# Seven products for a part of z, behind the first feed-forward, and new stage offsets

## The chip, the cores and the metric

The kernel runs on one NeuronCore of a Trainium2 chip. A core has TensorE (PE, matmuls), VectorE (DVE), ScalarE (ACT), GpSimd (POOL) and SyncE (SP, which issues nearly all transfers here), each with its own instruction stream, kept in step by semaphores. The metric is the time of one execution on the device in microseconds, the median of several.

## The reference

One layer of a decoder trunk over 2048 tokens of width 1024, in fp32: a gated DeltaNet mixer of 8 heads beside a memory cross-attention of 4 heads, then a squared-ReLU feed-forward, with a layer norm behind each. What matters for the change is the projection z, the gate of the mixer:

```python
def gdn_mixer(x, mem_k, mem_v, w_in, conv_w, a_log, dt_bias, gate_norm_w, w_out):
    proj = x @ w_in                                  # x: 2048 x 1024
    qkv = proj[..., :3 * GDN_WIDTH]
    z = proj[..., 3 * GDN_WIDTH:4 * GDN_WIDTH]       # 1024 columns, 128 to a head
    ...
    qkv = jax.nn.silu(causal_depthwise_conv(qkv, conv_w))
    ...
    o = chunk_gated_delta_rule(q, k, v, g, beta)     # state carried from chunk to chunk
    o = (rms_norm(o, gate_norm_w) * jax.nn.silu(heads(z))).reshape(B, T, GDN_WIDTH)
    m = memory_attention(mq, mem_k, mem_v)
    return jnp.concatenate([o, m], axis=-1) @ w_out

x = layer_norm(ALPHA * x + mix, ln1_g, ln1_b)
x = layer_norm(ALPHA * x + sqrelu_mlp(x, w_ff1, w_ff2), ln2_g, ln2_b)
```

z doesn't depend on the recurrence, so it can be computed at any time before the gate is applied.

## The kernel before

**Precision.** Every large product is made of three matmuls in fp32r: each operand is split into a high and a low part (ACT casts the high part, DVE subtracts it for the low one), and `mm3` adds high x high, high x low and low x high in PSUM. A wide matmul is 128 x 128 weights times 512 columns.

**Stages.** The 2048 tokens are four blocks of 512 (b = 0 to 3), and two blocks are a superblock (s = 0, 1). For each superblock the program runs the mixer of its two blocks, then the output projection (`out_seven`), the feed-forward's first half (`ff1`) and its second half (`ff2`). In the trace the first superblock takes from 0 to 1367 us, and its `ff2` from 1057 to 1367; the mixers of blocks 2 and 3 run from 1367 to 1942.

**Seven products.** `out_seven`, `ff1` and `ff2` multiply 2 x 2 blocks of matrices by seven products in place of eight (table `SEVEN`, L1190): sums and differences of the operands' quadrants (A11 to A22 and S1 to S4 of the tokens, B11 to B22 and T1 to T4 of the weights) are made by DVE beforehand, kept in DRAM, and loaded and split when their product comes. `quad_sums` (L1202) makes those of weights. In `ff2` each of the seven takes 192 wide matmuls (PSUM tiles f2A, f2B, f2C), in eight steps of 24; step u loads tokens (X, or xh and xl in the seventh product) and weights (whl).

**The mixer.** `mixer` (L1677) goes through ten steps t. Step t makes q, k and v of head t (`dense`: three projections of 24 wide matmuls, PSUM tiles aq, ak, av), the chunk-local part of head t-1 (`gdn_a`, `invert`: transposes ptk, ptq, ptv, products pkq, and the small products pq, pp in fp32), the recurrence of head t-2 (`gdn_b`: pc, po, pto), z of head t-1 (`gate`, L843: 24 wide matmuls into az, then tanh on ACT and one DVE instruction into cz), and in four steps a memory head (amq, sps, pmT, pmo). In blocks 1 to 3 the split weights are loaded from wsc in DRAM, where block 0 has put them. Between these, ACT, DVE and POOL do the convolution, the norms and the inverse.

**What sets the order.** The program is recorded, not issued, as it is written; `Recorder.issue` (L336) then lays all instructions out engine by engine. It gives each a cost and a time at which its operands would be ready, and at each point takes, of the instructions that could start, the one of the lowest priority number. That number is the place in the written order plus a stage offset from the table `PLACE` (`spot`, L552; `o.prio`, L245): (2, 4, 'Z') is z in step 4 of block 2. The chip then runs each engine's stream strictly in that order. SP is such a stream too: a transfer that waits for a free buffer holds up those behind it.

**Buffers that matter here.** Tag "d" has 11 tiles of 128 x 512, tag "s0" 14, whl 4 (each the high and low part of 128 x 1024), the token tiles "tt" 8; PSUM has 8 banks (acc 3, ga0, ga1, pb 2, m).

All instructions of the recorder have one line in the profile, L447, so rows are told apart by their tiles.

Of the kernel before, what the change touches and what calls it, by code (L numbers as in the profile page):

```python
# [14 lines left out]
P = 128  # L15
# [169 lines left out]
class Op:  # L185
# [278 lines left out]
def hybrid_layer(  # L464
# [378 lines left out]
    def gate(b, h, T):  # L843
        a = bank("az", "acc")
        project(a, load_in(b, ZO // P + h), T)
        c = slot("cz", "d")
        th = slot("th", "th")
        nc.scalar.activation(th, a, AF.Tanh, scale=0.5)
        nc.vector.scalar_tensor_tensor(out=c, in0=th, scalar=1.0, in1=a, op0=ALU.add, op1=ALU.mult)
        return c  # L850
# [327 lines left out]
    MEM_AT = {5: 0, 6: 1, 7: 2, 8: 3}  # L1178
# [320 lines left out]
    def ff2(s, x1d):  # L1499
# [58 lines left out]
        for n, (xn, wn, bn, on, (th, nh)) in enumerate(SEVEN):  # L1558
# [18 lines left out]
            for u in range(HU - LT):  # L1577
# [5 lines left out]
                if n == 3 and u in (2, 3):  # L1583
                    affine(*((ln2_g, "kq0"), (ln2_b, "kq1"))[u - 2])
                rec.gate = None
# [19 lines left out]
            if xn == "S1":  # L1605
                for t in range(NC):
                    norm2(NC + t)
# [331 lines left out]
```

## Time and profile before

| | us |
|---|---|
| Median of 3 runs | 2705.01 (2702.50 to 2705.70) |
| The profiled execution | 2702.34 |
| Its span, first to last instruction | 2700.6 |
| PE busy | 2685.2 (99%) |
| DVE busy | 2087.0 (77%) |
| ACT busy | 1624.8 (60%) |
| POOL busy | 423.3 (16%) |
| Bytes moved | 613.79 MB, mean 227 GB/s |
| Granted TensorE clock | 0.999 (2.4 GHz) |

The profile's busy share is a union of spans: two instructions that overlap in an engine's pipeline count once. A row of the timeline joins equal instructions that follow each other; its start, and the start of the next row, tell how long the run held the engine. A wait is listed with the engine that stood still, and with what ended it.

### The profile page before, as it was taken

The page shows a single profiled execution, that of the slowest core. Times are in us where ns is not written, and L with a number is a line of the kernel's source. Part 1 is how long each engine was busy: PE and PEld are TensorE (multiplying, and loading weights), DVE is VectorE, ACT ScalarE, POOL GpSimd, SP SyncE. Part 2 cuts the span into 40 slices and gives each one's busy share as a digit, 9 for nine tenths or more (in the row PEclk, how much of TensorE's full clock was granted, in tenths as well). Part 3 has the DMA queues.
Part 4 walks back from the last instruction along what each step waited for, and adds up shares of the span by engine and source line. Part 5 has one row for each costly group of instructions (what it writes and reads, how often), then busy time and mean ns, then how long its engine had stood idle before and what let it go on. Part 6 is the DMA issues. An engine that isn't in the chain of part 4 may idle for free.

```text
span 2700.6 us, 42393 instructions
## 1 busy us (share of the span) xinstructions
PE 2685.2 (99%) x13577; PEld 2248.5 (83%) x13577; DVE 2087.0 (77%) x5604; ACT 1624.8 (60%) x4098; POOL 423.3 (16%) x1023
## 2 busy tenths in 40 slices
PE   9999999999999999999999999999999999999998
PEld 7888888888888888888888888888887888888887
DVE  7998889998867776756778888789977656667575
ACT  7778777776575555334446776578756655544341
POOL 3333133331000000000032221233201000000001
PEclk9999999999999999999999999999999999999999
DMA  8676659868788888765664444444678644586673
GB/s 317 235 258 207 234 178 311 300 233 285 276 307 289 293 302 287 270 215 189 234 222 157 151 150 175 175 162 138 238 271 290 206 138 153 171 293 216 215 237 114
DMA packets 209070, 613.79 MB, mean 227 GB/s; under 512 B 24112, under 2 KB 32720, under 8 KB 188880
## 3 DMA queue, kind: packets, MB, share of 16 engines
q1 hardware_dynamic: 208416, 611.04, 65.0%
q8 instruction: 107, 1.75, 0.3%
q14 instruction: 115, 0.94, 0.1%
q10 hardware_dynamic: 432, 0.05, 0.0%
HBM read 436.35 MB, written 174.65 MB: 226 GB/s over the span
## 4 chain that ended last, share of the span: by engine, by line
PE 96%; DVE 2%; ACT 1%; DMA 0%; issue 0%; POOL 0%; POOLq 0%; ACTq 0%; DVEq 0%
PE f2A L447 13%; PE fA L447 13%; PE ao L447 8%; PE az L447 7%; PE fC L447 6%; PE f2C L447 6%; PE av L447 6%; PE ak L447 6%; PE aq L447 6%; PE fB L447 3%; PE f2B L447 3%; PE amq L447 3%; PE pc L447 3%; PE po L447 2%; PE pkq L447 2%; PE pq L447 1%
## 5 line engine op out<-in xcount | busy, mean ns | idle before, releaser
L447 DVE TENSOR_TENSOR whl<-wraw,whl 128x512 fp32r<-128x512 f32 (+2 forms) x294 | 256.9, 884 | 102.6 <-ACT whl L447 99.9
L447 ACT CAST whl<-wraw 128x512 fp32r<-128x512 f32 (+2 forms) x294 | 226.2, 780 | 182.6 <-PE fC L447 73.5
L447 PE MATMUL fA<-B,whl 128*128 128x512 f32 x1152 | 286.4, 389 | 0.0
L447 PE MATMUL f2A<-whl,X 128*128 128x512 f32 x1152 | 263.1, 389 | 0.0
L447 ACT CAST X<-X 128x1024 fp32r<-128x1024 f32 x118 | 124.1, 1052 | 228.1 <-DMA X<-xsc 174.6
L447 PEld LDWEIGHTS fA<-B,whl 128*128 128x128 f32 x1152 | 216.2, 188 | 45.0
L447 PEld LDWEIGHTS f2A<-whl,X 128*128 128x128 f32 x1152 | 216.3, 188 | 44.9
L447 DVE TENSOR_TENSOR X<-X,X 128x1024 fp32r<-128x1024 f32 x118 | 143.8, 1221 | 130.2 <-ACT X L447 130.0
L447 PE MATMUL az<-T,whl 128*128 128x512 f32 x768 | 215.9, 406 | 0.0
L447 PE MATMUL ak<-T,whl 128*128 128x512 f32 x768 | 213.4, 405 | 0.6 <-ACT cq L447 0.5
L447 PE MATMUL aq<-T,whl 128*128 128x512 f32 x768 | 210.6, 404 | 0.5 <-DVE T L447 0.4
L447 PE MATMUL av<-T,whl 128*128 128x512 f32 x768 | 209.3, 403 | 0.0
L447 PE MATMUL fC<-B,whl 128*128 128x512 f32 x768 | 196.9, 389 | 0.0
L447 PE MATMUL f2C<-whl,X 128*128 128x512 f32 x768 | 174.7, 389 | 0.0
L447 PEld LDWEIGHTS fC<-B,whl 128*128 128x128 f32 x768 | 144.1, 188 | 30.1 <-DVE B L447 0.2
L447 PEld LDWEIGHTS f2C<-whl,X 128*128 128x128 f32 x768 | 144.2, 188 | 29.9
L447 POOL TENSOR_SCALAR ve<-mv 128x1 f32<-128x1 f32 x34 | 15.6, 460 | 915.0 <-DVE mv L447 915.0
L447 PEld LDWEIGHTS aq<-T,whl 128*128 128x128 f32 x768 | 136.7, 189 | 25.3 <-DVE T L447 2.3
L447 PEld LDWEIGHTS ak<-T,whl 128*128 128x128 f32 x768 | 137.1, 189 | 24.3 <-ACT cq L447 0.6
L447 PEld LDWEIGHTS av<-T,whl 128*128 128x128 f32 x768 | 137.4, 189 | 23.2
L447 PEld LDWEIGHTS az<-T,whl 128*128 128x128 f32 x768 | 136.5, 189 | 22.4
L447 PE MATMUL ao<-whl,X 128*128 128x512 f32 x528 | 139.7, 403 | 0.0
(296 smaller groups left out, 6260.8 us busy)
## 6 DMA issues: line engine op xcount, KB each, us to landing
whl<-wsc SPq DMA_DIRECT2D x108, 1024.0 KB, 4.9
wraw<-in_w_ff_dram SPq DMA_DIRECT2D x106, 512.0 KB, 4.3
X<-xsc SPq DMA_DIRECT2D x96, 512.0 KB, 3.9
wsc<-whl SPq DMA_DIRECT2D x36, 1024.0 KB, 6.0
whl<-tsc SPq DMA_DIRECT2D x64, 512.0 KB, 4.8
xsc<-hB SPq DMA_DIRECT2D x96, 256.0 KB, 3.1
xo<-cat SPq DMA_DIRECT2D x80, 256.0 KB, 3.3
wraw<-in_w_in_dram SPq DMA_DIRECT2D x35, 512.0 KB, 5.9
```

What stands on the lines that cost most here:

```text
L447: o.fn(*[res(a) for a in o.args], **{k: res(v) for k, v in o.kw.items()})
```

## The change

Three things change.

1. z of heads 0 to 3 in blocks 2 and 3 is no longer made in the mixers. The tokens of blocks 2 and 3 (th = 0, 1) are the rows, and heads 0, 1 and 2, 3 (nh = 0, 1) the columns of a 2 x 2 problem, with the 1024 inputs halved; seven products of 24 wide matmuls make it, in a new function `gate_seven` that stands behind the first superblock's `ff2`. Its gated result goes to DRAM (zsc), and `gate` in the mixers loads it from there.
2. The sums that it needs are made in `ff2` of the first superblock, at six places (`SUMS_AT`) in its third, fourth and fifth product: of weights into zws, of tokens into zxs.
3. The table of stage offsets is another one throughout. The memory heads of block 3 stand one step later (`MEM_AT`), the first weights of block 2 are loaded behind `gate_seven`, and the last norms of `ff2`'s second half have small offsets.

```diff
@@ PLACE: 176 offsets before, 215 now, nearly all with other values
-    ('w',): 140, (0, 0, 'D'): 5, (0, 0, 'F'): -5, (0, 0, 'H'): -585, (0, 1, 'D'): -70, (0, 1, 'F'): 75,
+    (None,): 190, ('w',): 70, (0, 0, 'D'): 50, (0, 0, 'H'): -210, (0, 1, 'D'): -225, (0, 1, 'H'): 145,
...
     def gate(b, h, T):
+        if b in Z_BLOCKS and h < 2 * ZH:
+            c = slot("cz", "d")
+            nc.sync.dma_start(out=c, in_=zsc[b, h])
+            return c
         a = bank("az", "acc")
...
-    MEM_AT = {5: 0, 6: 1, 7: 2, 8: 3}
+    MEM_AT = {b: {5 + (b == 3) + h: h for h in range(MH)} for b in range(NB)}
...
@@ in ff2, before step u of product n
+                if s == 0 and (n, u) in SUMS_AT:
+                    spot(n, u, "zS")
+                    i = SUMS_AT.index((n, u))
+                    (gate_weight_sums if i < ZH else gate_token_sums)(i if i < ZH else i - ZH)
+                    spot(None)
...
             if xn == "S1":
                 for t in range(NC):
+                    rec.shift = 30 + 45 * t
                     norm2(NC + t)
+                rec.shift = 0
...
+    Z_BLOCKS = (2, 3)
+    ZH = 2
+    SUMS_AT = ((2, 0), (2, 4), (3, 0), (3, 3), (3, 6), (4, 1))
...
+    def gate_token_sums(k):
+        a11, a12, a21, a22 = (slot("xq", "d") for _ in range(4))
+        for b, lo, hi in zip(Z_BLOCKS, (a11, a21), (a12, a22)):
+            for x, kk in ((lo, k), (hi, k + KT // 2)):
+                nc.sync.dma_start(out=x, in_=xtd[:, kk, b * TB:(b + 1) * TB])
+        nc.sync.dma_start(out=zxs["A22"][:, k].part(k), in_=a22)
+        sub(a22, a21, a22, ALU.add)
+        sub(a21, a11, a21)
+        sub(a11, a22, a11)
+        sub(a12, a12, a11)
+        for n, x in (("S1", a22), ("S3", a21), ("S2", a11), ("S4", a12)):
+            nc.sync.dma_start(out=zxs[n][:, k].part(k), in_=x)
...
+    def gate_seven(T):
+        K2 = KT // 2
+        def tokens(n):
+            if n in ("A11", "A12"):
+                ks = range(K2 * (n == "A12"), K2 * (n == "A12") + K2)
+                return [(T_of(T, 0, k), T_of(T, 1, k)) for k in ks]
+            x = []
+            for k in range(K2):
+                hi, lo = slot("xh", "d", F32R), slot("xl", "s0", F32R)
+                split_in_place(hi, lo, zxs[n][:, k].part(k))
+                x.append((hi, lo))
+            return x
...
+        def finish(th, nh, j, a, c):
+            g = slot("th", "th")
+            nc.scalar.activation(g, a, AF.Tanh, scale=0.5)
+            nc.vector.scalar_tensor_tensor(out=c, in0=g, scalar=1.0, in1=a, op0=ALU.add, op1=ALU.mult)
+            nc.sync.dma_start(out=zsc[Z_BLOCKS[th], nh * ZH + j], in_=c)
...
+        for n, (xn, wn, bn, on, q) in enumerate(SEVEN):
+            spot(n, 0, "zX")
+            x = tokens(xn)
+            spot(n, 0, "zW")
+            w = weights(wn)
+            spot(None)
...
+            for j in range(ZH):
+                a = banks[bn][j]
+                for k in range(K2):
+                    c = slice(k * P, (k + 1) * P)
+                    mm3(a, w[j][0][:, c], w[j][1][:, c], *x[k], k == 0 and not on, k == K2 - 1, skip_group_check=on)
+                if q == (0, 1):
+                    finish(*q, j, a, slot("cz", "d"))
+                elif (q, j) not in met:
...
+                    nc.scalar.copy(out=held[q, j], in_=a)
+                else:
+                    sub(held[q, j], a, held[q, j], ALU.add)
+                    finish(*q, j, held[q, j], held[q, j])
...
         ff2(s, x1d)
+        if s == 0:
+            gate_seven(ahead["T"])
+            ahead["w0"] = load_in(Z_BLOCKS[0], 0)
```

What this does to the order is seen at three places. The first is PE at the end of the first superblock's `ff2`: f2A is its last product, T the split tokens of block 2 (two numbers, high and low), aq the first projection of block 2's mixer, az a product of z. Before:

```order
L447 MATMUL f2A<-whl,xh 128x512 x2
L447 MATMUL f2A<-whl,xl 128x512
L447 MATMUL aq<-T_14640,whl 128x512
L447 MATMUL aq<-T_14652,whl 128x512
L447 MATMUL aq<-T_14640,whl 128x512 x2
```

And now, with a piece left out in which the first product goes on:

```order
L454 MATMUL f2A<-whl,xh 128x512 x2
L454 MATMUL f2A<-whl,xl 128x512
L454 MATMUL az<-T_14761,whl 128x512
L454 MATMUL az<-T_14771,whl 128x512
L454 MATMUL az<-T_14761,whl 128x512 x2
...
L454 MATMUL az<-xh,whl 128x512
L454 MATMUL az<-xl,whl 128x512
```

Where the mixer began, z begins: first on the tokens T, then on the loaded sums xh and xl. 147 of its 168 matmuls stand in one run; the other 21, of the seventh product, stand between the first two heads' projections.

The second place is SP at the same stage: xl is a token tile as it lands, whl weights, xj and wraw are what the next block's tokens and the feed-forward's weights land in. Before:

```order
L447 DMA xj<-in_xt_dram 128x512 x2
L447 DMA whl<-wsc 128x2048
L447 DMA xl<-xsc 128x512 x8
L447 DMA wraw<-in_w_ff_dram 128x1024
L447 DMA xj<-in_xt_dram 128x2x512 x3
L447 DMA scr<-gct 32x128
```

And now:

```order
L454 DMA xl<-xsc 128x512 x8
L454 DMA xl<-zxs 128x512 x2
L454 DMA xj<-in_xt_dram 128x2x512
...
L454 DMA whl<-wsc 128x512 x4
L454 DMA xl<-zxs 128x512
L454 DMA scr<-gct 32x128
L454 DMA out_dram<-y 128x512 x2
L454 DMA xl<-zxs 128x512
L454 DMA whl<-zws 128x1024
```

Seven token loads for the seven products stand between the feed-forward's last token loads and the weights of the first product; the others follow, among writes of the output.

The third is PE in block 2's mixer, where head 0's z stood: ptk and ptq are transposes of a head's k and q. Before:

```order
L447 MATMUL az<-T_14694,whl 128x512
L447 MATMUL ptk<-ident,ck 128x128 x4
L447 MATMUL az<-T_14683,whl 128x512 x2
...
L447 MATMUL az<-T_14823,whl 128x512
L447 MATMUL ptq<-ident,cq 128x128 x4
L447 MATMUL az<-T_14817,whl 128x512 x2
```

And now:

```order
L454 MATMUL aq<-T_14793,whl 128x512
L454 MATMUL ptk<-ident,ck 128x128 x4
L454 MATMUL aq<-T_14802,whl 128x512
...
L454 MATMUL aq<-T_14929,whl 128x512
L454 MATMUL ptq<-ident,cq 128x128 x4
L454 MATMUL aq<-T_14935,whl 128x512
```

The transposes that stood among z's matmuls stand among the next head's first projection. In numbers of instructions over the whole program: PE 12495 before and 12471 now; DVE's TENSOR_TENSOR 2499 and 2553; ACT's casts and copies 1735 and 1765; SP's DMAs 1410 and 1506.

## Rows read from the trace of the kernel before

**Rows 1.** The page, busy us (share of the span) and instructions.

```profile
PE 2685.2 (99%) x13577; PEld 2248.5 (83%) x13577; DVE 2087.0 (77%) x5604; ACT 1624.8 (60%) x4098; POOL 423.3 (16%) x1023
```

**Rows 2.** The page, the chain that ended last, by engine.

```profile
PE 96%; DVE 2%; ACT 1%; DMA 0%; issue 0%; POOL 0%; POOLq 0%; ACTq 0%; DVEq 0%
```

**Rows 3.** Waits of PE: us in total, times, longest us.

```profile
PE ao L447 <- ACT whl L447: 1.4, 4, 0.6
PE warm L447 <- POOL mhalf L534: 1.2, 1, 1.2
...
PE pp L447 <- POOL at L447: 0.2, 1, 0.2
```

**Rows 4.** Windows: us, PE, PEld, DVE, ACT, POOL busy, clock, DMA share, GB/s.

```profile
0.00:310.00 310.00, 306.69 (x1710) 256.42 (x1710) 273.77 (x954) 240.58 (x709) 102.51 (x234) 1.00 0.72 254
310.00:610.00 300.00, 299.13 (x1740) 255.92 (x1739) 275.42 (x1083) 223.88 (x777) 99.31 (x244) 1.00 0.72 251
...
1057.00:1276.00 219.00, 219.00 (x968) 181.41 (x967) 132.49 (x141) 86.81 (x86) 2.85 (x6) 1.00 0.69 235
...
1367.00:1650.00 283.00, 283.00 (x1612) 241.46 (x1610) 231.85 (x923) 193.24 (x667) 81.85 (x232) 1.00 0.48 171
1650.00:1942.00 292.00, 291.71 (x1673) 249.32 (x1674) 248.00 (x982) 207.66 (x726) 85.30 (x213) 1.00 0.49 172
```

**Rows 5.** Timeline of PE in ff2: start us, us, instructions joined.

```profile
1189.52 43.68 PE L447 MATMUL f2C<-whl,X 128*128 128x512 f32 x192
1233.04 43.68 PE L447 MATMUL f2A<-whl,X 128*128 128x512 f32 x192
```

**Rows 6.** Timeline of PE in the mixer of block 2.

```profile
1377.65 5.60 PE L447 MATMUL av<-T,whl 128*128 128x512 f32 x24
1383.10 1.30 PE L447 MATMUL aq<-T,whl 128*128 128x512 f32 x5
...
1402.28 1.98 PE L447 MATMUL az<-T,whl 128*128 128x512 f32 x8
1404.10 0.60 PE L447 MATMUL ptk<-ident,ck 128*128 128x128 f32 x4
1404.46 3.03 PE L447 MATMUL az<-T,whl 128*128 128x512 f32 x12
1407.33 0.60 PE L447 MATMUL ptq<-ident,cq 128*128 128x128 f32 x4
1407.68 1.17 PE L447 MATMUL az<-T,whl 128*128 128x512 f32 x4
1408.69 1.98 PE L447 MATMUL aq<-T,whl 128*128 128x512 f32 x8
```

**Rows 7.** Windows of three other stretches, columns as in rows 4.

```profile
490.00:520.00 30.00, 29.40 (x168) 24.93 (x166) 28.95 (x106) 21.62 (x70) 12.00 (x29) 1.00 0.95 351
1189.00:1232.00 43.00, 43.00 (x192) 35.60 (x191) 21.42 (x21) 16.54 (x16) 0.00 (x0) 1.00 0.67 220
...
1367.00:1400.00 33.00, 33.00 (x158) 27.64 (x157) 25.24 (x43) 19.91 (x60) 13.78 (x31) 1.00 0.78 304
```

**Rows 8.** Timeline of PE in out_seven of superblock 1, transposes.

```profile
2059.78 0.27 PE L447 MATMUL pt<-ident,y 128*128 128x128 f32 x1
...
2060.58 0.71 PE L447 MATMUL pt<-ident,y 128*128 128x128 f32 x5
```

**Rows 9.** DVE: z's gate from 1367 to 1942; the sums, ns min/median/max.

```profile
L447 DVE SCALAR_TENSOR_TENSOR cz<-th,az 128x512 f32<-128x512 f32 x16 | 10.9, 682 | 2.8 <-ACT th L447 2.7
L447 DVE TENSOR_TENSOR wq<-wq x88: 637/685/748, 308.3 to 1030.5; 128x512 f32<-128x512 f32 x88
```

**Rows 10.** Tile xl: cast, subtraction (ns min/median/max), landing.

```profile
L447 ACT CAST xh<-xl x68: 603/620/644, 644.3 to 2664.1; 128x512 fp32r<-128x512 f32 x68
L447 DVE TENSOR_TENSOR xl<-xl,xh x68: 642/686/694, 645.6 to 2664.8; 128x512 fp32r<-128x512 f32 x68
...
DMA to landing us min/median/max: 3.0/6.2/8.1
```

More of the change, by code (lines that the diff above doesn't have):

```diff
@@ L1606, in ff2 @@
                 for t in range(NC):
+                    rec.shift = 30 + 45 * t
                     norm2(NC + t)
+                rec.shift = 0
+    Z_BLOCKS = (2, 3)
+    ZH = 2
+    SUMS_AT = ((2, 0), (2, 4), (3, 0), (3, 3), (3, 6), (4, 1))
+    zsc = {(b, h): rec.buf(dr, (P, TB), F32, "zsc%d%d" % (b, h), 1, "zsc") for b in Z_BLOCKS for h in range(2 * ZH)}
+    zws = {n: rec.buf(dr, (P, ZH * TB), F32, "zws" + n, 1, "zws") for n in ("T1", "T2", "T3", "T4")}
+    zxs = {n: rec.buf(dr, (P, KT // 2, TB), F32, "zxs" + n, 1, "zxs") for n in ("S1", "S2", "S3", "S4", "A22")}
@@ new lines, in gate_weight_sums @@
+    def gate_weight_sums(j):
+        w = [w_in[ZO // P + j + ZH * nh] for nh in range(2)]
+        quad_sums([slot("wq", "d") for _ in range(4)],
+                  {(h, nh): w[nh][:, h * TB:(h + 1) * TB] for h in range(2) for nh in range(2)},
+                  {n: zws[n][:, j * TB:(j + 1) * TB] for n in zws}, 0)
+    def gate_token_sums(k):
[10 more added lines that the diff above has]
+            nc.sync.dma_start(out=zxs[n][:, k].part(k), in_=x)
@@ new lines, in gate_seven, with weights @@
+    def gate_seven(T):
[10 more added lines that the diff above has]
+            return x
+        def weights(n):
+            w = []
+            for jp in range(ZH // 2):
+                t, hi, lo = pair()
+                if n[0] == "T":
+                    split_in_place(hi, lo, zws[n][:, jp * 2 * TB:(jp + 1) * 2 * TB].part(2 * jp, 2 * jp + 1))
+                else:
+                    h, nh = int(n[1]) - 1, int(n[2]) - 1
+                    for i in range(2):
+                        for u, v in enumerate((hi, lo)):
+                            c = slice(u * 1024 + h * TB, u * 1024 + (h + 1) * TB)
+                            nc.sync.dma_start(out=v[:, i * TB:(i + 1) * TB].bitcast(F32),
+                                              in_=wsc[ZO // P + 2 * jp + i + ZH * nh][:, c])
+                w += [(hi[:, i * TB:(i + 1) * TB], lo[:, i * TB:(i + 1) * TB]) for i in range(2)]
+            return w
+        def finish(th, nh, j, a, c):
[3 more added lines that the diff above has]
+            nc.sync.dma_start(out=zsc[Z_BLOCKS[th], nh * ZH + j], in_=c)
+        tags = {"A": ("ga0", "ga1", "pb", "pb"), "B": ("acc", "acc", "acc", "m")}
+        tags["C"] = tags["B"]
+        banks, held, met = {}, {}, set()
+        for n, (xn, wn, bn, on, q) in enumerate(SEVEN):
[4 more added lines that the diff above has]
+            spot(None)
+            if not on:
+                banks[bn] = [bank("az", g) for g in tags[bn]]
+            for j in range(ZH):
[6 more added lines that the diff above has]
+                elif (q, j) not in met:
+                    met.add((q, j))
+                    if j % 2 == 0:
+                        t = tok_tile("z")
+                        for i in range(2):
+                            held[q, j + i] = t[:, i * TB:(i + 1) * TB].part(i)
+                    nc.scalar.copy(out=held[q, j], in_=a)
+                else:
+                    sub(held[q, j], a, held[q, j], ALU.add)
+                    finish(*q, j, held[q, j], held[q, j])
@@ L1672, in next_block @@
         else:
-            ahead["w0"] = load_in(b, 0)
+            if b != Z_BLOCKS[0]:
+                ahead["w0"] = load_in(b, 0)
             ahead["G"] = gates(b, ahead["ab"])
@@ L1695, in mixer @@
             spot(b, t, "M")
-            if t in MEM_AT:
-                h = MEM_AT[t]
+            if t in MEM_AT[b]:
+                h = MEM_AT[b][t]
                 c = cat_tile()
```

67 rows, old and new, of the table PLACE are left out of this document.

## The prediction

> **What bounds the kernel now.** I read the page's busy times first [rows 1]: PE is busy 2685.2 us of 2700.6, DVE comes next with 77%. The chain of waits says the same in another way [rows 2]: 96% of what ended last is PE. The waits of PE alone [rows 3] are ten entries that add up to 6.6 us; the remaining idle time, 15.4 - 6.6 = 8.8 us, is the last normalisation after the last product. So PE hardly ever stands still, and what shortens the kernel is fewer or cheaper PE instructions, or up to 6.6 us of waits.
>
> The windows by stage [rows 4] show who is second where. In the mixers of blocks 2 and 3 (1367 to 1942) PE idles 0.29 us of 575 and DVE is busy 231.85 + 248.00 = 479.85 us, 83%. In the mixers of blocks 0 and 1, DVE is at 88% and 92%, and PE idles 3.31 and 0.87 us. So a mixer can run with 92% of DVE and still cost PE only 0.3% of its time. In the feed-forward's second half DVE is at 60%.
>
> A busy PE need not be PE at its peak, so the price of a matmul is read from starts. An unbroken run of 192 products starts at 1189.52 and the next group at 1233.04 [rows 5]: 43.52 / 192 = 0.2267 us for one matmul of 512 columns. In a mixer a run of 24 goes from 1377.65 to 1383.10 [rows 6], 0.227 again. PE is at its own rate in both places; the 83% of PEld [rows 1] is what such a run shows as well (35.60 of 43.00 us, [rows 7]).
> The Trainium skill (Trace Analysis, section Identifying the Most-Contended Engine) says that matmul occupancy is a bad measure of headroom and that the busy share of weight loads should be used; by that 17% of PE would be free, the removed matmuls would sit on spare time, and the result would be 2702.3 us, no gain. The unbroken run with 83% of weight loads disagrees: there is no hole in it to take up, so I go by the rows and keep the rule as a small rival.
>
> **The change, part by part.**
> 1. Removed on PE: z of heads 0 to 3 in blocks 2 and 3 is 2 x 4 x 8 x 3 = 192 matmuls; the seven products are 7 x 2 heads x 4 x 3 = 168. That is 24 x 0.2267 = -5.44 us. They all are on the path, since PE is.
> 2. New order on PE. I counted in the two orders how often PE goes back from small fp32 products to the wide ones: 709 times before, 736 now. Price of one: head 0's z in block 2 starts at 1402.28 and the next projection at 1408.69 [rows 6]; within these 6.41 us stand 24 wide matmuls (5.45) and two groups of four transposes, so a group costs 0.48. Five transposes in a row take 0.71 and one 0.27 [rows 8], so one more costs 0.11 and four cost 0.44. An interruption itself is 0.04 us; 27 x 0.04 = +1.1 us. Bounds: 0, and 27 x 0.48 = 13 if the whole group were extra work, which it isn't, because the number of transposes is the same.
> 3. Added to DVE and ACT, behind the first superblock's feed-forward. DVE gets 54 more subtractions: 24 for the sums of weights and tokens (0.685 each as the wq rows, [rows 9]), 20 splits of tokens (0.69, [rows 10]), 4 splits of weights at twice that width, and 6 joins; about 40 us in all. ACT gets 30 casts and copies, about 20 us. The 24 sums (16 us) fall in the second half of the feed-forward, where DVE has 86 us free [rows 4]. The rest, 24 us, and the 8 gates of z that come here from the mixers (8 x 0.682, [rows 9]) fall beside 38.1 us of seven products (168 x 0.2267). In the 33 us that follow the feed-forward now, DVE was busy 25.24 [rows 7]; together 55 of 71 us. Hidden. Were it not hidden, the whole 29 us could show.
> 4. The mixers of blocks 2 and 3 lose 192 x 0.2267 = 43.5 us of PE work as cover and only 8 x 0.682 of DVE's [rows 9]. DVE then is busy 474.4 of 531.5 us, 89%. Between the two mixers that show 88% and 92% [rows 4]: block 1's idle share, 0.29%, gives 1.5 us of idle, block 0's (with the program's start in it) 5.7. I take 1.5, which is +1.2 on the 0.29 us there now. The order supports it: the transposes of k and q that stood among z's matmuls stand among the next head's aq now, with 12 wide matmuls between them, as before.
> 5. Added DMAs: 96 on SP. Of these, 52 are the sums, 13.6 MB within about 100 us from the third of the seven feed-forward products on. The stretch moves 220 GB/s now [rows 7], so it will ask for about 350. The seven products load 5.2 MB of tokens, 5.2 MB of weights and store 2.1 MB, 12.5 MB; with the 10 MB of the 33 us that follow now (304 GB/s, [rows 7]) that is 22.5 MB in 71 us, 317 GB/s. The mixer stretch at 490 us moves 351 GB/s with PE idle 0.60 of 30 us [rows 7]: 2% of idle is the nearest row, 2 us over the first stretch if its look-ahead weren't there. The token loads of the feed-forward run four steps ahead of PE (tag "tt", eight buffers, two a step), so I take 0, and keep the 2 us as an end.
> The Trainium skill (DMA: Bandwidth & Descriptors, section Specifications) puts HBM's limit at about 358 GB/s for a core; by it the first stretch would just fit, which changes no term. The trace's 351 GB/s over 30 us is in accord.
> 6. SP's queue. Between the last feed-forward loads and the first mixer weights now stand 20 token loads, each of which waits for a free slot. Tag "d" has 11 slots, 2.75 products of four. A load that is issued when a product ends has 1.75 x 5.44 = 9.5 us until its use. It needs 6.2 us to land (median; the longest 8.1), 0.62 on ACT and 0.69 on DVE [rows 10]: 7.5 us, 9.4 at worst. It fits by 2 us. Behind a late one wait the weights of the next product and, after them, of the first mixer.
> 7. The offsets elsewhere: the number of PE instructions in each other stage is the same, and only 6.6 us of PE waits are there to win or to double. I take 0, with -5 and +5 as ends.
>
> Sum: -5.4 + 1.1 + 1.2 = -3.1 us. The profiled execution took 2702.34 us (its span is 2700.6), so the sum gives 2699.2 on it. It lies below all three timed runs (2702.50 to 2705.70, median 2705.01); on their median the sum gives 2701.9. I forecast a median between these, nearer to the latter: 2701.4 us.
>
> **The rivals.**
> (a) The new offsets also recover waits. For it: 6.6 us of waits are listed, and no reason protects them. Against it: they are ten small entries, the longest 1.2 us, and at the program's start the order barely changes. With all of them halved, another -3.3 us: 2698; with all of them gone, 2695.
> (b) The cover is gone: with 43.5 us less PE work in the mixers, DVE sets their pace here and there. At block 0's idle share, 5.7 us come in place of 1.5, and the sum is +1.1: about 2706 on the median, no change. DVE at 100% isn't reached (474 of 531), so it can't be more by this way alone.
> (c) The seven products starve; this ends on the slower side. PE takes them in their written order, 147 z matmuls in one run, so a token tile that comes late stops PE with nothing to fill in. The place is the 38 us behind the feed-forward; the point from which it decides is a load-to-use time over 9.5 us. If the look-ahead shrinks to one product, each of the five products with token sums waits 7.5 - 5.4 = 2.1 us: +10.5. Then 2705.0 - 3.1 + 10.5 = 2712. For it: SP's queue is in order, and writes of the output that wait for the normalisation stand among these loads. Against it: the first product needs no loaded tokens, and seven of the token loads stand ahead of its weights.
> (d) The change doesn't do what it says: the wide matmuls sit on spare PE time, and nothing is gained. 2705. Only the weight-load share speaks for it.
>
> **How the numbers follow.** A measurement of this kernel can tell about 0.2% (5.4 us) from no change, so faster means under 2699.6 us and slower over 2710.4. The forecast (a gain of 1 to 6 us) has 0.55, of which 0.10 lie under 2699.6. Rival (a) has 0.22, nearly all faster. Rival (b) has 0.09, all within. Rival (c) has 0.11, nearly all slower. Rival (d) has 0.03. So faster 0.32, within 0.57, slower 0.11. Eight times in 10 the time should lie between 2694 (rival (a) with all the waits gone) and 2712 (rival (c)); the forecast's own range is 2698 to 2705.
>
> **What would show it.** Wide matmuls: 9960 in place of 9984, with the unbroken runs still at 0.2267. The stage behind the feed-forward: seven products in about 38 us with no PE wait on xl, xh or whl; waits of 2 us there, about five, would be rival (c). Mixers 2 and 3 together, without the seven products: about 533 us, with DVE near 89% and PE idle under 2 us; 4 us or more would be rival (b). The ten PE waits: a total of 3 us or less would be rival (a). The prediction is wrong if the seven products end but the mixers don't get shorter by some 43 us, or if another stage, above all the first two mixers, moves by more than 3 us.

## The result, and the profile after

The changed kernel takes 2709.82 us, the kernel before 2703.55 us in the same session (medians of 12 runs each): a ratio of 1.0024, 95% interval 1.0016 to 1.0031, so 6.3 us slower where 2701.4 us and a small gain were forecast. One of the twelve executions took 10919.59 us, at a mean granted clock of 0.591; it is left out of the ratio. The profiled execution of the kernel after took 2714.14 us, 4.3 us over its median; what belongs to it alone is marked below.

The page after, busy times, to be held against [rows 1]:

```profile
span 2712.4 us, 42585 instructions
PE 2689.3 (99%) x13553; PEld 2243.7 (83%) x13553; DVE 2122.5 (78%) x5658; ACT 1638.8 (60%) x4128; POOL 425.5 (16%) x1023
```

PE has 24 instructions fewer and is "busy" 4.1 us longer. It also idles 23.1 us in place of 15.4. Its waits (us in total, times, longest us), cf. [rows 3]:

```profile
PE pto L454 <- ACT on L454: 2.7, 1, 2.7
PE av L454 <- DVE whl L454: 2.2, 1, 2.2
PE ptv L454 <- ACT Y L454: 1.3, 5, 0.5
PE warm L454 <- POOL mhalf L541: 1.2, 1, 1.2
...
PE fC L454 <- DVE B L454: 0.7, 2, 0.4
PE fA L454 <- DVE B L454: 0.7, 2, 0.5
```

And the chain that ended last, by engine, cf. [rows 2]:

```profile
PE 91%; DVE 4%; ACT 2%; DMA 1%; POOL 1%; issue 1%; POOLq 0%; ACTq 0%; SPq 0%; DVEq 0%
```

Five per cent of the chain have left PE. The windows of the kernel after, columns as in [rows 4]: mixer 1, the seven products with the first head of block 2, the rest of mixer 2, mixer 3, and the second output projection.

```profile
315.40:619.10 303.70, 299.91 (x1727) 253.90 (x1726) 275.92 (x1103) 222.52 (x763) 99.16 (x238) 0.99 0.71 250
...
1378.00:1433.10 55.10, 55.10 (x246) 45.33 (x245) 36.14 (x53) 29.04 (x58) 7.34 (x15) 1.00 0.86 308
1433.10:1672.60 239.50, 239.29 (x1381) 204.03 (x1380) 203.26 (x812) 174.88 (x615) 75.00 (x208) 1.00 0.45 161
1672.60:1945.40 272.80, 272.60 (x1608) 232.60 (x1607) 249.06 (x1036) 204.44 (x729) 84.23 (x218) 1.00 0.48 168
1945.40:2086.60 141.20, 138.25 (x690) 112.61 (x690) 115.69 (x251) 78.38 (x169) 12.52 (x28) 1.00 0.78 273
```

The second output projection in the kernel before:

```profile
1941.80:2079.20 137.40, 135.75 (x677) 113.06 (x676) 110.96 (x227) 78.31 (x158) 11.36 (x24) 1.00 0.78 276
```

The stage of the seven products has no idle PE, and mixers 2 and 3 idle 0.4 us. Mixer 1, which has no part in the change of z, idles 3.8 us ([rows 4] of before: 0.9), and the second output projection 3.0 (1.65 before).

Idle time is only the visible part, since waits of a fraction of an instruction vanish in "busy". So I price each PE instruction at the median distance, in the kernel before, from its start to the next start for the same three kinds of instruction in a row. The sum over a stage is its work; what the stage took beyond that is called its waits here; what matmuls lose at a lower granted clock is among them. Both, in us, for the profiled executions (e-numbers are the experiments below):

| stage | before | after | e1 | e5 | e6 | e8 | e10 |
|---|---|---|---|---|---|---|---|
| mixer 0 | 11.7 | 15.4 | 11.4 | 11.8 | 11.6 | 12.2 | 11.4 |
| mixer 1 | 5.2 | 10.7 | 9.3 | 5.3 | 4.4 | 5.3 | 5.2 |
| output projection 0 | 2.1 | 2.4 | 2.4 | 2.3 | 2.6 | 2.0 | 2.3 |
| feed-forward 0, first half | -0.1 | 1.3 | 1.5 | 2.3 | 1.3 | -0.3 | -0.1 |
| feed-forward 0, second half | -0.2 | -0.2 | -0.2 | 1.2 | -0.2 | -0.2 | -0.2 |
| seven products, mixers 2 and 3 | 7.0 | 8.1 | 9.8 | 8.3 | 6.9 | 8.3 | 8.7 |
| output projection 1 | 3.1 | 6.6 | 11.5 | 5.0 | 5.4 | 4.6 | 4.1 |
| feed-forward 1, first half | -0.3 | 1.2 | 2.7 | 1.2 | 1.2 | 0.6 | 0.3 |
| feed-forward 1, second half | -0.5 | -0.5 | -0.5 | -0.5 | -0.5 | -0.5 | -0.5 |
| all waits | 28.0 | 45.1 | 48.0 | 36.9 | 32.7 | 32.0 | 31.2 |
| all work | 2662.6 | 2657.6 | 2664.6 | 2657.4 | 2657.6 | 2658.2 | 2662.6 |

The work fell by 5.0 us, about as forecast. The waits rose by 17.1. On the medians that is -5.0 + 11.3 = +6.3. The difference between 17 and 11 lies mostly in mixer 0: its 15.4 (with the 2.2 us wait of av) is 11.4 to 12.1 in three other kernels with the same offsets there (e1, e6, e7), so that rise was of one execution. What is left stands in mixer 1 (+5.5), the second output projection (+2 to +3.5) and both first halves of the feed-forward (+1.4, +1.5); the stages that the seven products touch give +1.1.

Part of these waits is slower matmuls and not standing still. Behind the two longest waits of the list, the 2.2 us for whl and the 2.7 us for `on`, the granted clock of TensorE is 0.50 (1.2 GHz) for a stretch (windows of the kernel after):

```profile
25.75:29.16 3.41, 3.41 (x9) 2.65 (x8) 3.41 (x9) 1.02 (x2) 0.00 (x0) 0.50 1.02 366
449.00:452.42 3.42, 2.83 (x10) 2.46 (x11) 0.82 (x4) 3.25 (x12) 1.48 (x4) 0.50 0.24 90
```

In the kernel before the granted clock stays at 1.00 until 2695 us, behind its last matmul. What the first stretch costs is seen in the run of av behind the first wait (timeline of PE):

```profile
24.51 5.29 PE L454 MATMUL av<-T,whl 128*128 128x512 f32 x15 [2.21 <-DVE whl L454]
29.64 0.62 PE L454 MATMUL aq<-T,whl 128*128 128x512 f32 x2
```

From 24.51 to 29.64 go 15 wide matmuls, 5.13 us where 15 x 0.2267 = 3.40 would do: 1.7 us, and with the wait 3.9, which is the whole rise of mixer 0. The second stretch, in mixer 1, costs 1.1 us against the same matmuls in e6.

The largest single wait stands in mixer 1. Timeline of PE, GpSimd, ScalarE and VectorE of the kernel after (start us, us, what; in brackets the idle time before and what ended it):

```profile
444.61 2.30 PE L454 MATMUL az<-T,whl 128*128 128x512 f32 x9
449.59 0.47 PE L454 MATMUL pto<-ident,on 128*128 128x128 f32 x1 [2.68 <-ACT on L454]
```

```profile
443.51 0.18 POOL L454 COPY halo<-raw 128x3 f32<-128x3 f32 x1
443.65 5.48 POOL L454 TENSOR_TENSOR ro<-m,mhalf 128x4 f32<-128x4 f32 x1
449.11 0.64 POOL L454 TENSOR_SCALAR_AFFINE_SELECT dl<-gb 128x512 f32<-128x512 f32 x1
```

```profile
444.89 1.15 ACT L454 ACTIVATE vb<-ptv,vbs 128x128 f32<-128x128 f32 x4 [0.75 <-PE ptv L454]
449.17 1.14 ACT L454 ACTIVATE on<-po,ro 128x128 f32<-128x128 f32 x4 [3.13 <-POOL ro L454]
```

```profile
443.84 0.68 DVE L454 TENSOR_TENSOR kq<-ck,kq 128x512 fp32r<-128x512 f32 x1
444.44 0.16 DVE L454 TENSOR_TENSOR Bc<-Bc,Lc 128x8 f32<-128x8 f32 x1
444.52 0.74 DVE L454 SCALAR_TENSOR_TENSOR cv<-raw,cw,cv 128x512 f32<-128x512 f32 x1
...
445.93 0.16 DVE L454 STREAM_SHUFFLE Bc<-Xc 128x12 f32<-128x12 f32 x1
446.00 0.74 DVE L454 SCALAR_TENSOR_TENSOR cv<-raw,cw,cv 128x512 f32<-128x512 f32 x1
...
447.49 0.74 DVE L454 SCALAR_TENSOR_TENSOR cv<-raw,cw,cv 128x512 f32<-128x512 f32 x1
```

In the kernel before the same power took 1.05 us:

```profile
L447 POOL TENSOR_TENSOR ro<-m,mhalf x1: 1047/1047/1047, 436.9 to 436.9; 128x4 f32<-128x4 f32 x1
```

PE waits for `on`, `on` for the power `ro`, and the power takes 5.48 us, 4.4 more than before. From 443.84 to 448.23, 4.39 us, VectorE runs one instruction behind the other without a gap, nearly all with two operands in SBUF; the power ends 0.9 us behind that row, about its usual length. In the kernel before no GpSimd instruction takes over 2 us. The load of transfers isn't it: before, the power took 1.05 us while the DMA engines were fully busy (371 GB/s from 434 to 440 us), and the kernel after has 322 GB/s from 443 to 449. The Trainium skill (SBUF — State Buffer, section SBUF: two separate sides) says that a VectorE operation with two SBUF inputs and a GpSimd operation that reads SBUF need the same pair of ports, that the lock on it is exclusive, and that the loser is blocked fully. The 5.48 us agree with that; a short shuffle with one operand within the row (0.16 us at 445.93) did not let the power through.

### The profile page after: what moved, and what is told of

The parts are those of the page before. It is cut to its first block, busy times and chain, and to the rows that moved or that the text cites. A ratio compares the mean times of both kernels' runs of the same rounds, so it can differ in the third digit from the quotient of the medians.

```text
span 2712.4 us, 42585 instructions
## 1 busy us (share of the span) xinstructions
PE 2689.3 (99%) x13553; PEld 2243.7 (83%) x13553; DVE 2122.5 (78%) x5658; ACT 1638.8 (60%) x4128; POOL 425.5 (16%) x1023
## 3 DMA queue, kind: packets, MB, share of 16 engines
q1 hardware_dynamic: 222240, 630.97, 66.3%
## 4 chain that ended last, share of the span: by engine, by line
PE 91%; DVE 4%; ACT 2%; DMA 1%; POOL 1%; issue 1%; POOLq 0%; ACTq 0%; SPq 0%; DVEq 0%
PE f2A L454 13%; PE fA L454 13%; PE ao L454 7%; PE f2C L454 6%; PE fC L454 6%; PE av L454 6%; PE az L454 6%; PE ak L454 6%; PE aq L454 5%; PE f2B L454 3%; PE fB L454 3%; PE amq L454 3%; PE pc L454 3%; PE po L454 2%; PE pkq L454 2%; PE pq L454 1%
## 5 line engine op out<-in xcount | busy, mean ns | idle before, releaser
L454 PE MATMUL av<-T,whl 128*128 128x512 f32 x768 | 220.7, 409 | 2.2 <-DVE whl L454 2.2
L454 PE MATMUL az<-T,whl 128*128 128x512 f32 x624 | 175.6, 408 | 0.0
L454 ACT CAST whl<-whl 128x1024 fp32r<-128x1024 f32 x92 | 96.8, 1052 | 95.1 <-DMA whl<-wos 44.7
```

What stands on the lines that cost most here:

```text
L454: o.fn(*[res(a) for a in o.args], **{k: res(v) for k, v in o.kw.items()})
```

## The experiments

Theory: the redrawn offsets of stages without any part in the seven products cost about 11 us of waits; the seven products bring 5. Main rival: the sums, loads and stores of the seven products cost it.

**e1: the offsets alone.** The kernel before with the other kernel's table.

```diff
 PLACE = {
-    ('w',): 140, (0, 0, 'D'): 5, (0, 0, 'F'): -5, (0, 0, 'H'): -585, (0, 1, 'D'): -70, (0, 1, 'F'): 75,
+    (None,): 190, ('w',): 70, (0, 0, 'D'): 50, (0, 0, 'H'): -210,
...
```

> The kernel before with only the redrawn stage offsets: no seven products, z of heads 0 to 3 of blocks 2 and 3 stays in the mixers. Theory (the new offsets cost PE waits in stages that the seven products don't touch, about 11 us, and the seven products themselves bring about -5 us): about 2703.5 + 11 = 2714 us, 2710 to 2718, with the added waits in the first two mixers and in the second superblock's output projection. Rival (the seven products with their sums, loads and stores cost the time, the redraw is neutral): 2703.5 us, at most 2 us from the kernel before. Second rival (the redraw costs something only together with the seven products, because it was drawn for them): 2703.5 again in the first superblock, waits in blocks 2 and 3 alone.

Measured: 2724.39 us, ratio 1.0078 (1.0065 to 1.0091). Both rivals fall: without any product the offsets cost 21 us, in mixer 1 (+4.1), the second output projection (+8.4) and the first halves of the feed-forward (+4.6). Of the +8.4, about 2.7 are lost at a granted clock of 0.50 from 2041.8 to 2048.6, which begins within a wait of 2.4 us for whl. The wait of 2.6 us for `on` in mixer 1 is there too, but the clock stays at 1.00 behind it, and mixer 1 has 9.3 us in place of 10.7. The size was twice that expected. The power in mixer 1 takes 5.48 us here too. PE's first waits, columns as above:

```profile
PE pto L454 <- ACT on L454: 4.2, 2, 2.6
PE ao L454 <- DVE whl L454: 2.7, 2, 2.4
PE ptv L454 <- ACT Y L454: 1.7, 5, 0.5
```

**e2: the seven products alone.** OLD and NEW are the tables of the two kernels; 190 is what NEW adds to everything without a label.

```diff
     def spot(*key):
-        rec.base = PLACE.get(key, 0)
+        rec.base = NEW.get(key, 0) - 190 if (len(key) == 3 and key[2] in ('zX', 'zW', 'zS')) else OLD.get(key, 0)
...
-    MEM_AT = {b: {5 + (b == 3) + h: h for h in range(MH)} for b in range(NB)}
+    MEM_AT = {b: {5 + h: h for h in range(MH)} for b in range(NB)}
...
-                    rec.shift = 30 + 45 * t
```

> The kernel after with the old offsets under every label that the kernel before has, the old places of the memory heads, and the old order of the last standardisations; only the three new labels (operands, weights and sums of the seven products) keep their new offsets. Theory: the seven products bring 5 us and the old offsets add no wait in the first superblock: about 2698.5 us, 2696 to 2702. Rival (the seven products cost the time): 2709 us or more, with PE waits in the stage behind the first feed-forward or in mixers 2 and 3. Second rival (the old offsets don't fit blocks 2 and 3 without z of heads 0 to 3): 2702 to 2707, with new PE waits in mixers 2 and 3 alone.

Measured: 2734.48 us, 1.0112 (1.0097 to 1.0128). My theory fell in this form, and the first rival has the number. The work is 5.3 us less, but the waits are 66.3 us: +11.1 in mixer 3, +14.1 in the second output projection, +7.5 in the second half of the first feed-forward, +2.6 in mixer 2. In mixer 1 they are 5.3, as before. Some 9 us of the 66.3 are lost at a granted clock of 0.50, in five stretches of 23.9 us in all, each behind one or several listed waits. That the products themselves aren't at fault in mixers 2 and 3 is shown by e3, which has them and waits 7.8 us there. So the old offsets don't do for a program without z in the mixers, nor the new ones (e1) for one with it: blocks 2 and 3 had to be redrawn.

**e3: new offsets for mixers 2 and 3 and the seven products only** (the last standardisations in their old order, as in e2).

```diff
-        rec.base = PLACE.get(key, 0)
+        rec.base = NEW.get(key, 0) - 190 if (len(key) == 3 and (key[2] in ('zX', 'zW', 'zS') or key[0] in (2, 3) and key[2] in 'BADZMYKO')) else OLD.get(key, 0)
```

> The kernel after with the new offsets only in mixers 2 and 3 and at the seven products, and the old ones in mixers 0 and 1, in both output projections and in both feed-forwards. Theory: the first superblock's mixers and the second superblock's output projection lose their added waits: about 2699 us, 2696 to 2702, faster than both kernels. Rival (the seven products cost the time): about 2709 us. Second rival (each stage's waits hang on the order of the whole, so that mixing two sets of offsets makes waits of its own): 2704 to 2712.

Measured: 2710.95 us, 1.0028 (1.0017 to 1.0040): in the second rival's range. Mixer 1 is back at 5.5 us and mixers 2 and 3 at 7.8, as the theory has it, but the second half of the first feed-forward waits 6.2 us. Timelines of PE and VectorE of e3 there:

```profile
1282.61 2.43 PE L488 MATMUL f2B<-whl,X 128*128 128x512 f32 x10
1289.54 1.90 PE L488 MATMUL f2B<-whl,X 128*128 128x512 f32 x4 [4.50 <-DVE X L488]
```

```profile
1285.02 1.41 DVE L488 SCALAR_TENSOR_TENSOR y<-y,mv,l2kq 128x512 f32<-128x512 f32 x2
1286.34 1.41 DVE L488 SCALAR_TENSOR_TENSOR y<-y,rs,l2kq 128x512 f32<-128x512 f32 x2
1287.67 0.69 DVE L488 BATCH_NORM_STATS2 bn<-y 128x6 f32<-128x512 f32 x1
1288.27 1.21 DVE L488 TENSOR_TENSOR X<-X,X 128x1024 fp32r<-128x1024 f32 x1
```

The split of X stands behind a row of normalisations on VectorE. Its spare time in that stage hides the added sums only if the order leaves the splits ahead. The 6.2 us are this wait of 4.5 and about 1.5 at a granted clock of 0.50 behind it (1289.8 to 1293.1). They don't speak for the second rival's reason: the matmuls and splits of `ff2` have no labels of their own, and e2 and e3, which have the sums and leave out the delays of the last standardisations (`rec.shift`), are the only runs with this wait. The kernel before, e1 and e10 lack the delays too, but have no sums there. That the delays keep the splits ahead is therefore the likelier cause; it isn't shown, since no two runs differ by them alone.

**e4: old offsets in mixers 0 and 1 only.**

```diff
-        rec.base = PLACE.get(key, 0)
+        rec.base = NEW.get(key, 0) - 190 if (not (len(key) == 3 and key[0] in (0, 1) and key[2] in 'BADZMYKO')) else OLD.get(key, 0)
```

> The kernel after with the old offsets in mixers 0 and 1 alone, new ones everywhere else. Theory: mixers 0 and 1 lose the 9 us by which their waits rose in the profiled execution, of which 2.2 us (a wait of DVE for a DMA at the start) may be of that execution alone: 2709.8 - 7 = about 2703 us, 2701 to 2705. Rival (the second superblock's output projection and the two feed-forwards carry most of it): 2707 to 2710 us.

Measured: 2709.18 us, 1.0021 (1.0012 to 1.0030), the rival's number, yet not for its reason: mixer 1's waits are 5.3 us again, and the gain is lost at the seam, 5.3 us in the first output projection (2.4 in the kernel after) and 3.8 in the feed-forward behind it (1.3).

**e5: old offsets in the first superblock up to its second feed-forward half.**

```diff
-        rec.base = PLACE.get(key, 0)
+        rec.base = NEW.get(key, 0) - 190 if (key[-1] in ('zX', 'zW', 'zS') or len(key) == 3 and key[0] in (2, 3) and key[2] in 'BADZMYKO' or key[-1] in ('H', 'w') or key[0] == 1 and key[-1] in ('n', 'X', 'W', 'F')) else OLD.get(key, 0)
```

> The kernel after with the old offsets in all of the first superblock up to its second feed-forward half (mixers 0 and 1, output projection, first half of the feed-forward), new ones from there on. Theory: the waits of mixer 1 (10.7 us in the kernel after, 5.2 before) and of the first feed-forward half (1.3, and -0.1 before) go back, and those at the seam that the mixed version with old offsets in the two mixers alone showed (5.3 us in the output projection, 3.8 in the feed-forward) don't arise: about 2709.8 - 6.5 = 2703 us, 2702 to 2705. Rival (a set of offsets is only good as a whole, and a seam costs wherever it lies; then it moves to the second feed-forward half or the seven products): 2707 to 2711 us. Second rival (the second superblock alone carries the loss): 2708 to 2710.

Measured: 2707.05 us, 1.0013 (1.0004 to 1.0022), at the near edge of the rival's range. Mixer 1 is repaired (5.3), and the seam shows again, smaller: 2.3 us in the first half of the feed-forward and 1.2 in the second. Of the 6.3 us, 3.7 are gone (+2.6 against its own runs of before).

**e6: VectorE's backlog taken away, order unchanged.**

```diff
                     nc.vector.scalar_tensor_tensor(out=c, in0=raw[:, j:j + TB], scalar=cw[:, j * 24 + gi:j * 24 + gi + 1],
                                                    in1=c, op0=ALU.mult, op1=ALU.add)
+                    if j == 1 and b in (1, 3):
+                        f = rec.ops[-1].fn
+                        rec.ops[-1].fn = lambda f=f, **kw: f(**{k: v[:, :2] if k in ("out", "in0", "in1") else v
+                                                                for k, v in kw.items()})
```

> The kernel after in exactly its own order on every engine, but the second of the three convolution taps that VectorE adds is done on 2 columns in place of 512 in blocks 1 and 3 (24 instructions of 0.66 us each and block, 16 us a block; the output is then not the reference's). Theory (PE's added waits in mixer 1 and in the second output projection are for results that VectorE's backlog makes late, directly, or through ScalarE and GpSimd that wait for it): PE's waits in mixer 1 fall from 10.7 to about 6 us, those of the second output projection from 6.6 to about 3, and the time by about 7 us, to 2703. Rival (the order itself puts a product too close behind the ScalarE or GpSimd work that it needs, and VectorE is not the one who is late): both stay as they are, 2708 to 2710. Between the two: if VectorE's unbroken row of instructions with two operands in SBUF is what holds GpSimd's power (5.48 us in place of 1.1) up, the 2.7 us wait for it in mixer 1 gets shorter by some 1.3 us (two taps are in that row), whatever becomes of the rest.

Measured: 2702.51 us, 0.9993 (0.9985 to 1.0002). Mixer 1's waits fall from 10.7 to 4.4 us, as the theory says; the second output projection stays at 5.4, against it. Timelines of GpSimd and of VectorE in this kernel, the power and the end of the row beside it:

```profile
439.03 3.26 POOL L454 TENSOR_TENSOR ro<-m,mhalf 128x4 f32<-128x4 f32 x1
```

```profile
441.38 0.20 DVE L884 SCALAR_TENSOR_TENSOR cv<-raw,cw,cv 128x2 f32<-128x2 f32 x1
441.51 0.16 DVE L454 TENSOR_TENSOR Bc<-Bc,Lc 128x12 f32<-128x12 f32 x1
441.59 0.20 DVE L884 SCALAR_TENSOR_TENSOR cq<-raw,cw,cq 128x2 f32<-128x2 f32 x1
...
441.80 0.74 DVE L454 SCALAR_TENSOR_TENSOR cv<-raw,cw,cv 128x512 f32<-128x512 f32 x1
```

PE's wait for `on`, and the clock around it (windows of e6):

```profile
PE pto L454 <- ACT on L454: 0.5, 1, 0.5
```

```profile
441.00:452.00 11.00, 10.54 (x60) 8.65 (x59) 9.09 (x36) 8.98 (x33) 3.43 (x5) 1.00 0.69 246
```

The power is 2.2 us shorter and PE waits 0.5 us for `on` in place of 2.7. It ends 0.25 us before VectorE's row does, so it got in at the short instructions and not only behind the row. The clock stays at 1.00: the 14 matmuls from the first pto on take 2.83 us here (442.75 to 445.58) and 3.88 in the kernel after (449.59 to 453.47). So of the 6.3 us that mixer 1 gains, some 1.1 are the clock.

**e7: part of ScalarE's work of block 3 taken away, order unchanged.** `cut()` makes the instruction recorded last work on 2 columns if the block is 3.

```diff
                 nc.scalar.activation(th, c, AF.Tanh, scale=0.5)
+                cut()
                 nc.vector.scalar_tensor_tensor(out=c, in0=th, scalar=1.0, in1=c, op0=ALU.add, op1=ALU.mult)
+                cut()
...
             nc.scalar.activation(j, p3[:, c], AF.Square, accum_out=o[:, c:c + 1])
+            cut()
...
                 nc.scalar.activation(pr[j][:, t], pr[j][:, t], AF.Copy, scale=rc[:, t:t + 1])
+                cut()
```

> The kernel after in exactly its own order on every engine, but in block 3 some ScalarE work is done on 2 columns in place of the whole width: the tanh behind the convolution (24, and the VectorE instruction that applies it), the squares of the output's norm (32) and the scaling of the memory heads' probabilities (8); the output is then not the reference's. Theory (the added waits of the second output projection, 5.0 to 6.6 us in the runs with this order and 3.1 before, are for ScalarE, which still works off mixer 3 there): they fall to 3 us or less, the time by some 2 to 4 us, to about 2706. Rival (they are loads and weight splits that the order puts too late, so no engine's backlog): they stay at 5 us and more; the run with VectorE's shortened taps left them at 5.4.

Measured: 2708.33 us, 1.0016 (1.0007 to 1.0024); the second output projection waits 5.6 us. The rival holds as far as this goes: neither the shortened part of VectorE's work of mixer 3 nor that of ScalarE's is what PE waits for there. What it is instead wasn't taken apart; the list of the kernel after names splits of whl and X for 1.6 of the 3.0 us there. Mixer 1, untouched here, is a second execution of the same order as the kernel after's: 11.0 us of waits, a granted clock of 0.50 behind the wait (447.7 to 451.0), and the power again (timeline of GpSimd)

```profile
440.34 5.48 POOL L454 TENSOR_TENSOR ro<-m,mhalf 128x4 f32<-128x4 f32 x1
```

**e8, e9 and e10: a third set of offsets, with and without the seven products.** Mixers 0 and 1 keep the old ones. The others were changed step by step, keeping what the kernel's ordering program takes for shorter. Some of e8's:

```diff
 PLACE = {
-    (None,): 190, ('w',): 70, (0, 0, 'D'): 50, (0, 0, 'H'): -210,
+    (0, 0, 0, 'W'): 590, (0, 0, 0, 'X'): 115, (0, 0, 1, 'W'): 450, (0, 0, 1, 'X'): -240, (0, 0, 2, 'W'): -450,
...
```

> The kernel after with the old offsets in mixers 0 and 1 and a third set of offsets everywhere else, searched with the kernel's own ordering program from the set of the run with the old first superblock. Theory (the seven products are worth their 5 us of matmuls, and what the kernel after lost is lost by offsets alone): waits at about those of the kernel before, 2700 us, 2697 to 2703, faster than both kernels. Rival (z made elsewhere takes cover from mixers 2 and 3 and costs waits there or behind them, whatever the offsets): 2704 to 2708, waits of 33 us or more in all.

> As the run before, from another start of the search (the old offsets in the second halves of both feed-forwards too). Theory: 2700 us, 2697 to 2703. Rival: 2704 to 2708.

> The kernel before, without the seven products, with the same search over the same labels (old offsets in mixers 0 and 1). It tells what the search brings by itself. Theory: waits stay near 28 us, 2701 to 2704, and the two kernels with the seven products are 1 to 5 us below it. Rival (the search brings the gain, the seven products nothing): it ends level with them.

Measured: e8 2701.54 us (2700.60 to 2702.97), 0.9991 (0.9982 to 1.0000); e9 2701.56 us, 0.9993 (0.9984 to 1.0002); e10 2705.44 us (2704.45 to 2709.58), 1.0008 (0.9999 to 1.0017). With offsets that fit, the same seven products end 8.3 us below the kernel after and some 2 below the kernel before, which is at the edge of what can be told. The clearer comparison is within the session: e8 and e9 lie 3.9 us below e10, which has no seven products and the same search, and no run of e8 reaches one of e10. The search by itself brought nothing (e10 is 1.4 us over its expected range); it was run once without the products, so how much of the 3.9 us is its luck isn't known. In the traces e8 has 4.4 us less work than e10 and 0.8 us more waits; e9's waits, 33.1 us, touch the rival's number, its time doesn't. e8's page, busy times, and PE's first waits:

```profile
span 2699.8 us, 42581 instructions
PE 2683.9 (99%) x13553; PEld 2241.7 (83%) x13553; DVE 2121.0 (79%) x5658; ACT 1635.3 (61%) x4128; POOL 421.6 (16%) x1023
```

```profile
PE pt L467 <- ACT st L467: 1.4, 2, 1.1
PE ao L467 <- ACT whl L467: 1.3, 3, 0.6
PE warm L467 <- POOL mhalf L554: 1.2, 1, 1.2
```

PE's busy time is 5.4 us below that of the kernel after, with the same 13553 instructions: that much of the "busy" there was waiting, or matmuls at half the clock (some 2.8 us by the two stretches above; e8 has its clock at 1.00 until 2695 us, behind its last matmul).

## Why the prediction was wrong

**Step 7 failed**: "only 6.6 us of PE waits are there to win or to double. I take 0, with -5 and +5 as ends." On the medians the waits rose by about 11 us, nearly all in stages that this step covered; that the offsets make them and not the seven products is shown by e8 and e9, which keep the products and end 8 us lower. Two things were wrong in it. The 6.6 us are the waits that the list shows; by starts, the kernel before has 28.0. And a stock of waits bounds a gain, not a loss: e1 adds 20 us, e2 38. That the number of PE instructions in a stage is the same says nothing about whether their operands are there. Nor does the step have a price for what follows a long wait, the halved clock. My condition for being wrong (another stage, above all the first two mixers, moves by more than 3 us) is what happened, in mixer 1. That the time still lies in the wide range, 2694 to 2712, is luck: its upper end was rival (c), which didn't happen.

**Steps 1 and 2 were right.** 24 wide matmuls less and more returns to the wide ones: -4.3 us forecast, -5.0 measured in the priced work. The unbroken runs go on at the old rate [rows 5], and 147 of the seven products' 168 matmuls take 33.58 us in a row, 0.228 each, as the chain of the kernel after in order of time shows (start us, us, what):

```profile
1070.28 43.52 PE f2A L454 x192
1113.80 43.52 PE f2C L454 x192
...
1378.13 33.58 PE az L454 x147
```

**Steps 3, 5 and 6 were right for this order.** The stage of the seven products has waits of 0.2 us, none of them long enough to be listed, so rival (c), the one on the slower side, didn't happen. One reading of step 5 is too narrow: the kernel before moves 404 GB/s from 1366.8 to 1383.1, more than the 358 that it cites, so the agreement at 351 is of that row alone; no term hung on it. e3 shows that "hidden" in step 3 hung on the order: with the normalisations ahead, VectorE's splits come 4.5 us late.

**Step 4 was right**: +1.2 us forecast for mixers 2 and 3 and +0.9 measured in the priced waits (VectorE at 88% of 512.3 us); idle PE, in which the step was worked out, is 0.4 us there and not 1.5. Rival (b) is refuted. Rival (a) named the right place with the wrong sign: the offsets did move waits, upwards. Rival (d) is refuted by the priced work.

Of the added waits, those in mixer 1 are shown to come from VectorE's backlog: 2.2 us through GpSimd's held-up power, some 1.1 through the clock that fell behind that wait (e6). Those in the first halves of the feed-forward are listed as waits for VectorE's splits of B (fA and fC, 0.7 us each); no run took them apart. The 2 to 3 us in the second output projection stay open: e6 and e7 exclude VectorE's and ScalarE's shortened work of mixer 3. Why the repair of mixer 1 didn't pay in full is shown by e4 and e5: where old and new offsets meet, waits arise that neither kernel has.

The sum without step 7, -3.1 us, is close to what the seven products bring: -3.9 with the same search on both sides (e8 and e9 against e10), -2.1 against the kernel before.

## What to carry to other kernels

Where a bound engine has no slack and takes its instructions in a fixed order, every redrawn order is a term of its own, and the listed waits of before are no bound for its loss. Price the bound engine by starts, stage by stage: "busy" took in some 5 us of waiting and of a halved clock here, and the list of waits another part. Look at the granted clock behind each long wait of TensorE: 2.2 and 2.7 us of standing still cost 1.7 and 1.1 us more here, though e1 had a wait of 2.6 without it. An offset table belongs to the program that it was drawn for; test an algorithmic change and its redraw apart, and give both programs the same redraw before comparing.

## What was not expected of the hardware

A GpSimd power on 128x4 that takes 1.05 us took 5.48 us beside an unbroken row of 4.39 us of VectorE instructions, the same in three kernels with that row (after, e1, e7; 5.480 to 5.483), and 3.26 us where two instructions of the row were cut to 2 columns (e6). No kernel with the old offsets in mixer 1 has a GpSimd instruction over 2 us. The ordering program of the kernel has no term for it.
